# Pinning weight casts, weight differences and splits behind the operation traced last, and q and k evictions by ScalarE first

## The chip, the core and the metric

The kernel runs on one core of a Trainium2 chip. The metric is the time of one execution in microseconds, taken as the median of several runs. One execution is also recorded by the hardware profiler. The engines are PE (TensorE, matrix products), ACT (ScalarE), DVE (VectorE), POOL (GpSimd) and SP (SyncE, which here only starts transfers). PE's weight loads are shown as PEld.

## The reference

One decoder layer over 1024 tokens with 16 learned tokens ahead of them, so 1040 rows of 1024 numbers. In its core:

```python
a = rmsnorm(h, ln_mix_pre)
dq, dk, dv, hq, hf, hi, hg = split(a @ w_in)          # seven groups of 512 columns
y_diff = diff_attention(dq, dk, dv, ...)              # 4 heads, two softmax maps each, blocks of 128
y_hgrn = hgrn2(hq, hf, hi, hg, ...)                   # 4 heads, gated linear recurrence
h = h + rmsnorm(concat(y_diff, y_hgrn) @ w_out, ln_mix_post)
a = rmsnorm(h, ln_ffn_pre)
y = (gelu(gate) * up) @ w_down   # gate, up = depthwise conv of a @ w_up, width 3
h = h + rmsnorm(y, ln_ffn_post)
```

All is float32.

## The kernel before

**Three products for one.** Each float32 matrix product is made of three: both operands are split into a high part (`wh`, `ahi`: a cast to a narrower format) and the rest (`wl`, `alo`: the operand less its high part), and PE computes high by high, high by low, low by high. `split` (line 154) does it for weights: ACT casts, and POOL, or DVE where it is named, subtracts. `load_split` (line 158) starts a transfer of 128 by 512 weights into one of three buffers `wr` and splits it into `wh` and `wl`, of which there are four each.

**Order.** PE executes in the order in which the program is traced. The order on ACT, DVE, POOL and SP's queue is made by a planner: it walks the traced program with its own estimate of the durations, and an engine that comes free gets the earliest traced operation whose inputs it thinks ready. An operation that is ready early can thus be hoisted far ahead of what was traced before it. `tc.issue_after(x)` forbids that: what is traced inside on x's engine is put behind x in that engine's order. `V` and `A` are wrappers of DVE and ACT (class `Ordered`, line 46) which keep traced order in a few parts of the program; `G` is POOL itself.

**The stages.** From about 11 us the first projections begin. Up to about 530 us PE works through the columns of `w_in`, one tile of 128 columns after another, mixed with attention and HGRN: for each head h a stretch of four tiles for HGRN (`hf`, `hq`, `hi`, `hg`) beside attention of head h, then a stretch of three tiles for attention of head h + 1 (`dq`, `dk`, `dv`) beside HGRN of head h. `interleave` (line 60) does the mixing: it first takes 1500 units of dense work, then, for each piece of the side work, dense work worth a number of units; a matmul of 384 columns counts 161 units. When the side work is done, the rest of the dense work follows alone. A stretch is one call of `dense` (line 741). For each tile it calls `load_m`, that is, `load_split` twice, for the next tile; for the first tile of a stretch it calls it at the stretch's beginning. A tile has three groups of columns (272, 384 and 384 tokens), each of 24 matmuls into one of two PSUM banks `pi_...` (lines 232, 234, 236: the third product needs `wl`, the first two need only `wh`), and after each group an eviction:

- `ev_q`, `ev_k` (lines 593, 598): ACT and DVE write the two 64-row halves of q and k in turn, with their low parts.
- `ev_v`: ACT copies to `vt`, which is transposed (`to_nat`, `pn_va`) in the group after, when `flush` is called at the group's step 8. `ev_i` does the same with `ht` (`pn_vh`).
- `ev_g`: a sigmoid, which is ACT exponential, DVE minimum, ACT logarithm, ACT exponential on `sg`, then a DVE product for `gate`.

Attention (`attn`, line 611) takes blocks i of 128 tokens: `scores(i)`, `values(i)` (transposes `pt`, copies `at` and `az`) and `apply(i)` (products `pa`, line 709). HGRN (`hgrn_head`, line 402) has levels whose products `pl` (line 451) need DVE's products on `mix` and `kr`.

**Weight differences.** The down projection at the end uses seven products for eight, for which differences of quarters of `w_down` are needed. `down_sums` (line 187) makes them beside the stretches above: at each group `dense` takes one step of it. It loads four pieces `wd` (five buffers), subtracts four times on DVE and stores each to `tsc`, eleven times over.

**Output projection**, about 530 to 640 us: `out_first` (line 1013) multiplies the mixed rows by the first half of `w_out` and loads and splits the second half on the way (`load_wo(1, k)`, line 928, DVE subtracts), which a second pass uses later. HGRN of the last head runs beside it.

Of the kernel before, what the change touches and what calls it, by code (L numbers as in the profile page):

```python
# [9 lines left out]
F32 = mybir.dt.float32  # L10
# [3 lines left out]
ALU = mybir.AluOpType  # L14
# [12 lines left out]
NBLK = 9  # L27
# [18 lines left out]
class Ordered:  # L46
# [3 lines left out]
    def __getattr__(self, name):  # L50
        call = getattr(self.engine, name)

        def issue(*args, **kw):
            ins = call(*args, **kw)  # L54
            return self.tc.keep_in_program_order(ins) if self.state["ordered"] else ins

        return issue
# [29 lines left out]
def layer_kernel(ctx: ExitStack, tc: tile.TileContext, x, meta, table, lbl, gpre, gpost, win,  # L87
# [3 lines left out]
    V, A = Ordered(tc, nc.vector, state), Ordered(tc, nc.scalar, state)  # L91
    G, T, SY = nc.gpsimd, nc.tensor, nc.sync
# [52 lines left out]
    def ps_in(name):  # L145
        return pp.tile([P, 512], F32, tag="ip", name=name)

    def ps_m(name):
        return pp.tile([P, 512], F32, tag="m", name=name)
# [1 line left out]
    def ps_s(name):  # L151
        return pp.tile([P, 2, 512], F32, tag="S", name=name)

    def split(hi, lo, raw, eng=None):
        A.copy(hi, raw)
        (eng or G).tensor_tensor(lo, raw, hi.bitcast(F32), op=ALU.subtract)

    def load_split(src, name, where=None, bufs=4):
        raw = wp.tile([P, 512], F32, tag="wr", name=f"wr_{name}", bufs=3)
        hi = (where or wp).tile([P, 512], F32R, tag="wh", name=f"wh_{name}", bufs=bufs)  # L160
        lo = (where or wp).tile([P, 512], F32R, tag="wl", name=f"wl_{name}", bufs=bufs)
        last_load.append(SY.dma_start(raw, src))
        split(hi, lo, raw)
        return hi, lo

    def rstd_of(dst, ss, n):
# [20 lines left out]
    def down_sums():  # L187
        def load(k):
            with tc.issue_after(last_load[-1].ins):
                for nm, kk, half in (("11", k, 0), ("12", k, 1), ("22", k + NF // 2, 1), ("21", k + NF // 2, 0)):  # L190
                    b[nm] = wsp.tile([P, 512], F32, tag="wd", name=f"wd{nm}_{k}")
                    SY.dma_start(b[nm], wdown[P * kk: P * (kk + 1), 512 * half: 512 * (half + 1)])
            b["t3"] = wsp.tile([P, 512], F32, tag="wd", name=f"wd3_{k}")

        b = {}
        load(0)
        yield
        yield
        for k in range(NF // 2):
            for j, d, p_, q_ in ((2, "t3", "22", "12"), (0, "12", "12", "11"), (1, "22", "22", "12"), (3, "21", "21", "22")):  # L200
                V.tensor_tensor(b[d], b[p_], b[q_], op=ALU.subtract)
                with tc.issue_after(last_load[-1].ins):
                    SY.dma_start(tsc[j][P * k: P * (k + 1)], b[d])
                yield
            if k + 1 < NF // 2:
                load(k + 1)
                yield

    def up_raw(ft, nm):
# [7 lines left out]
    def load_m(m, name, where=None, bufs=4):  # L217
        return [load_split(win[m][:, 512 * c: 512 * (c + 1)], f"{name}_{c}", where, bufs) for c in range(2)]

    def proj_group(g, parts, name, evac):  # L220
        b0, b1 = GROUPS[g]
        t0, t1 = start(b0), start(b1 - 1) + P
        n = t1 - t0
        pt = ps_in(f"pi_{name}_{g}")
        for k in range(KD):
            yield from proj_step(pt[:, :n], parts, k, t0, t1, lambda: evac(g, b0, b1, t0, t1, pt[:, :n]))
# [171 lines left out]
    def flush():  # L398
        while late:
            to_nat(*late.pop(0))  # L400
# [183 lines left out]
    def attn_in(h):  # L584
        qs = [ap_.tile([P, L], F32R, tag=f"q{m}", name=f"q{m}_{h}") for m in range(2)]
        ks = [ap_.tile([P, L], F32R, tag=f"k{m}", name=f"k{m}_{h}") for m in range(2)]
        vn = ap_.tile([P, NBLK, P], F32, tag="avn", name=f"avn{h}")
        G.memset(vn[:, 0], 0.0)
        rr = ap_.tile([P, 256], F32, tag="rr", name=f"rr{h}")
        own = [slice(0, 64), slice(64, 128)]  # L590
        oth = [slice(64, 128), slice(0, 64)]

        def ev_q(g, b0, b1, t0, t1, pt):
            for m in range(2):
                A.mul(qs[m][own[m], t0:t1], pt[own[m]], 0.125)
                V.scalar_tensor_tensor(qs[m][oth[m], t0:t1], pt[own[m]], 0.125, qs[m][own[m], t0:t1].bitcast(F32), ALU.mult, ALU.subtract)

        def ev_k(g, b0, b1, t0, t1, pt):
            for m in range(2):
                A.copy(ks[m][own[m], t0:t1], pt[own[m]])  # L600
                V.tensor_tensor(kl[m][own[m], t0:t1], pt[own[m]], ks[m][own[m], t0:t1].bitcast(F32), op=ALU.subtract)
                A.copy(ks[m][oth[m], t0:t1], pt[own[m]])

        def ev_v(g, b0, b1, t0, t1, pt):
            vt = ap_.tile([P, 384], F32, tag="vt", name=f"vt{h}_{g}", bufs=1)
            A.copy(vt[:, : t1 - t0], pt)
            late.append((vn, vt, b0, b1, f"va{h}_{g}"))

        return (qs, ks, vn, rr), [(h, f"dq{h}", ev_q), (4 + h, f"dk{h}", ev_k), (8 + h, f"dv{h}", ev_v)]

    def attn(h, tens):
        qs, ks, vn, rr = tens
# [115 lines left out]
        for i in range(NBLK):  # L728
            if i + 2 < NBLK:
                ahead = scores(i + 2)  # L730
                yield next(ahead)
            yield from apply(i)
            if i + 2 < NBLK:
                yield from ahead
            if i + 2 == NBLK:
                yield 2
            if i + 1 < NBLK:
                yield from values(i + 1)
        carry.append(pend.pop("tail"))

    def dense(tiles, preload=None, side=iter(())):
        parts = preload
        for idx, (m, name, evac) in enumerate(tiles):
            if parts is None:
                parts = load_m(m, name)
            nxt = load_m(tiles[idx + 1][0], tiles[idx + 1][1]) if idx + 1 < len(tiles) else None
            for g in range(3):
                next(side, None)
                for step, c in enumerate(proj_group(g, parts, name, evac)):
                    if step == 8:  # L750
                        flush()
                    yield c
            parts = nxt
# [28 lines left out]
    pt = ps_m("pg")  # L782
# [80 lines left out]
    for c in range(2):  # L863
        raw = wp.tile([P, 512], F32, tag="wr", name=f"wr3_{c}", bufs=3)
# [60 lines left out]
    FIRST = (2, 3, 4, 5, 6, 7, 8, 1)  # L925
    kept = kpp.tile([P, 2, KD, P], F32R, tag="kept", name="kept")

    def load_wo(n, k):
        raw = wp.tile([P, 512], F32, tag="wr", name=f"wor{n}_{k}", bufs=3)
        last_load.append(SY.dma_start(raw, wout[P * k: P * (k + 1), 512 * n: 512 * (n + 1)]))  # L930
        if k < 2:
            where, tag, bufs = wp, ("wh", "wl"), 4
        elif n == 0 and k < KD - 1:
            where, tag, bufs = w0p, ("woh", "wol"), KD - 3
        else:
            where, tag, bufs = w1p, ("woh", "wol"), KD - 1
        hi, lo = (where.tile([P, 512], F32R, tag=t, name=f"{t}{n}_{k}", bufs=bufs) for t in tag)
        split(hi, lo, raw, V if n or k else G)
        return hi, lo

    def tok(i):
# [41 lines left out]
    wo = []  # L983
# [29 lines left out]
    def out_first():  # L1013
        pys = [ps_s(f"py0_{i}")[:, 0] for i in FIRST[:2]]
        for ks in ((0, 1), (2, 3)):
            for j in range(2):
                yield from out_part(sps[j], pys[j], wo0, ks[0] == 0, False, ks)
        sqs = [mix_split(i, 4, 7) for i in FIRST[:2]]
        for j in range(2):
            yield from out_part(sqs[j], pys[j], wo0, False, True)  # L1020
            if j == 0:
                sp_ = mix_split(FIRST[2], 0, 4)
            A.copy(y0[:, FIRST[j]], pys[j])
        for n, i in enumerate(FIRST[2:]):
            for k in ((0, 1), (2, 3), (4,), (5,), (6,), (7,))[n]:
                wo.append(load_wo(1, k))
            if n == 3:
                ahead.extend(mix_load(2, c) for c in range(4))
            py = ps_in(f"py0_{i}")
            sq_ = mix_split(i, 4, 7)  # L1030
            yield from out_part(sp_, py, wo0, True, False)
            if i != FIRST[-1]:
                sp_ = mix_split(FIRST[n + 3], 0, 4)
            yield from out_part(sq_, py, wo0, False, True)
            A.copy(y0[:, i], py)
        py = ps_in("py0_0")
        yield from out_meta(py, wo0, 7)
        A.copy(y0[:2, 0], py[:2])
        while 0 not in finished:
            yield None  # L1040
        for p in range(3):
            pre_last[p] = mix_split(p, 7, 8)
        for p in range(3):
            yield from out_last(p)
# [171 lines left out]
    for n, i in enumerate(order):  # L1216
# [5 lines left out]
        if i < 2:  # L1222
            m = (m0, kept)[i]
# [499 lines left out]
```

## Time and profile before

| | us |
|---|---|
| median of 3 runs | 1327.34 |
| lowest and highest | 1326.83, 1329.81 |
| profiled execution | 1325.77 |
| its span, first to last instruction | 1324.0 |

A row of waits reads: engine, tile and line that waited, the engine and tile that ended the wait, total us, times, longest. A row in order of time reads: start, duration, engine, line, operation, tile written `<-` tiles read, shape; in brackets the idle time of the engine before it and what ended it. All operations of ACT and DVE carry line L54, that of the wrapper, so they are told apart by their tiles. A PE matmul's duration includes its passage through the pipeline; the next one starts before it ends. PEclk is the clock granted to PE, 1.00 being full.

### The profile page before, as it was taken

How to read it: one execution, taken by the hardware profiler on the slowest of the kernel's cores; microseconds unless marked ns; L12 is line 12 of the kernel's file. 1: busy time of each engine (PE TensorE's matmuls, PEld its weight loads, DVE VectorE, ACT ScalarE, POOL GpSimd, SP SyncE). 2: the span in 40 equal slices, each digit the busy share in tenths (PEclk: the TensorE clock that was granted, in tenths of full speed). 3: DMA queues.
4: the chain of work that ended last, by engine and by line, in shares of the span. 5: the costliest groups of instructions: out<-in, count | busy, mean ns of one | idle time of the engine just before them, and what ended most of it. 6: DMA issues, size and time to landing. Idle time of an engine off the chain costs nothing.

```text
span 1324.0 us, 26317 instructions
## 1 busy us (share of the span) xinstructions
PE 1276.6 (96%) x10227; PEld 1181.8 (89%) x10227; DVE 912.8 (69%) x1589; ACT 689.4 (52%) x1670; POOL 413.5 (31%) x324
## 2 busy tenths in 40 slices
PE   6999999999999999999999799999999999999997
PEld 5898899989999999777899799999999998888886
DVE  7666557564756465834778777877787876697587
ACT  7465346535654565545665454554454454554454
POOL 3211211121202120112147567667667641010021
PEclk9999999999999999999999899999999999999999
DMA  6331323132311011835713222222222324964363
GB/s 217 109 127 61 101 94 132 56 129 77 124 44 35 33 33 46 262 114 182 242 41 112 84 84 76 92 80 82 81 89 76 105 85 166 343 222 156 107 207 120
DMA packets 84371, 153.07 MB, mean 116 GB/s; under 512 B 9571, under 2 KB 19843, under 8 KB 84246
## 3 DMA queue, kind: packets, MB, share of 16 engines
q1 hardware_dynamic: 84246, 151.39, 34.0%
q8 instruction: 80, 1.31, 0.4%
q14 instruction: 45, 0.37, 0.1%
HBM read 112.69 MB, written 38.67 MB: 114 GB/s over the span
## 4 chain that ended last, share of the span: by engine, by line
PE 71%; DVE 6%; DMA 3%; ACT 3%; issue 2%; POOL 1%; SPq 1%; DVEq 0%; ACTq 0%; POOLq 0%
PE pd L1534 5%; PE pd L1535 5%; PE pd L1533 5%; PE pb L1336 4%; PE pb L1337 4%; PE pb L1338 4%; PE pa L1337 2%; PE pa L1336 2%; PE pa L1338 2%; PE pa L709 2%; PE pc L1338 2%; PE pc L1337 2%; PE pc L1336 2%; PE py L970 2%; PE py L974 2%
## 5 line engine op out<-in xcount | busy, mean ns | idle before, releaser
L1336 PE MATMUL pb<-t,uh 128*128 128x258 f32 (+1 forms) x480 | 135.4, 282 | 10.7 <-DVE u L54 10.7
L1337 PE MATMUL pb<-t,uh 128*128 128x258 f32 (+1 forms) x480 | 135.1, 281 | 0.0
L1338 PE MATMUL pb<-t,ul 128*128 128x258 f32 (+1 forms) x480 | 134.9, 281 | 0.0
L1534 PE MATMUL pd<-wl,gh 128*128 128x512 f32 (+1 forms) x314 | 121.4, 386 | 0.5 <-DVE wl L54 0.5
L1535 PE MATMUL pd<-wh,gl 128*128 128x512 f32 (+1 forms) x314 | 120.6, 384 | 0.0
L1533 PE MATMUL pd<-wh,gh 128*128 128x512 f32 (+1 forms) x314 | 120.1, 383 | 0.0
L54 DVE SCALAR_TENSOR_TENSOR c<-uu,cwt,c 128x512 f32<-128x512 f32 x88 | 92.4, 1050 | 22.5 <-ACT c L54 21.9
L1291 POOL TENSOR_TENSOR c<-c,c 128x512 f32<-128x512 f32 x44 | 68.4, 1554 | 124.1 <-ACT c L54 118.1
L1336 PEld LDWEIGHTS pb<-t,uh 128*128 128x128 f32 x480 | 91.5, 191 | 11.3 <-DVE u L54 11.3
L1337 PEld LDWEIGHTS pb<-t,uh 128*128 128x128 f32 x480 | 91.6, 191 | 0.0
L1338 PEld LDWEIGHTS pb<-t,ul 128*128 128x128 f32 x480 | 91.4, 190 | 0.0
L1337 PE MATMUL pa<-t,uh 128*128 128x258 f32 (+1 forms) x320 | 89.8, 281 | 0.0
L1338 PE MATMUL pa<-t,ul 128*128 128x258 f32 (+1 forms) x320 | 89.7, 280 | 0.0
L1336 PE MATMUL pa<-t,uh 128*128 128x258 f32 (+1 forms) x320 | 89.7, 280 | 0.0
L54 DVE SCALAR_TENSOR_TENSOR c<-ug,cwt,c 128x512 f32<-128x512 f32 x88 | 87.6, 996 | 1.7 <-ACT c L54 1.1
L1338 PE MATMUL pc<-t,ul 128*128 128x256 f32 x320 | 88.3, 276 | 0.0
L1336 PE MATMUL pc<-t,uh 128*128 128x256 f32 x320 | 88.3, 276 | 0.0
L1337 PE MATMUL pc<-t,uh 128*128 128x256 f32 x320 | 88.3, 276 | 0.0
L1534 PEld LDWEIGHTS pd<-wl,gh 128*128 128x128 f32 x314 | 59.0, 188 | 13.6 <-DVE wl L54 1.6
L1533 PEld LDWEIGHTS pd<-wh,gh 128*128 128x128 f32 x314 | 58.9, 188 | 12.6
L1535 PEld LDWEIGHTS pd<-wh,gl 128*128 128x128 f32 x314 | 59.0, 188 | 11.5
L54 ACT ACTIVATE pb<-S,ast 128x528 f32<-128x528 f32 (+7 forms) x72 | 46.5, 647 | 39.1 <-DVE ast L54 38.9
(411 smaller groups left out, 4210.3 us busy)
## 6 DMA issues: line engine op xcount, KB each, us to landing
ra<-in_wup_dram SPq DMA_DIRECT2D x80, 256.0 KB, 2.7
wd<-in_wdown_dram SPq DMA_DIRECT2D x44, 256.0 KB, 4.2
tsc<-wd SPq DMA_DIRECT2D x44, 256.0 KB, 2.7
gsc<-c SPq DMA_DIRECT2D x44, 256.0 KB, 2.0
wi<-tsc SPq DMA_DIRECT2D x44, 256.0 KB, 2.8
gi<-gsc SPq DMA_DIRECT2D x33, 256.0 KB, 3.7
wi<-in_wdown_dram SPq DMA_DIRECT2D x33, 256.0 KB, 3.0
msc<-mm SPq DMA_DIRECT2D x21, 256.0 KB, 3.5
```

What stands on the lines that cost most here:

```text
L54: ins = call(*args, **kw)
L709: T.matmul(po[:, :P], w_, vn[:, j], start=(j == 0), stop=(j == i))
L970: T.matmul(py[:r], mh[:, j, :r], hi, start=(first and j == 0), stop=False)
L974: T.matmul(py[:r], ml[:, j, :r], hi, start=False, stop=(last and k == k1 - 1))
L1291: G.tensor_tensor(cg, cg, cu, op=ALU.mult)
L1336: T.matmul(pt, hi[:, s], th[:, k], start=(first and k == 0), stop=False, skip_group_check=True)
L1337: T.matmul(pt, hi[:, s], tl[:, k], start=False, stop=False, skip_group_check=True)
L1338: T.matmul(pt, lo[:, s], th[:, k], start=False, stop=(k == 3), skip_group_check=True)
L1533: T.matmul(py, gh[:, s], wh, start=(k == 0 and pr not in (3, 7)), stop=False, skip_group_check=True)
L1534: T.matmul(py, gh[:, s], wl, start=False, stop=False, skip_group_check=True)
L1535: T.matmul(py, gl[:, s], wh, start=False, stop=(k == NH - 1), skip_group_check=True)
```

## The change

- The wrapper remembers the operation traced last on its engine, and `in_turn(engine)` puts what is traced inside behind it in that engine's order.
- The ACT casts in `load_split` are pinned so; POOL's subtraction is not. `split` called from elsewhere is not pinned.
- The DVE subtractions of `down_sums` are pinned so, and after each load there is one more step before the next four.
- In `ev_q` both ACT scalings come before both DVE operations, in `ev_k` all four ACT copies before both DVE subtractions.
- In attention's last blocks there are more pauses, in which dense work is taken: one more unit before the last `apply`, and three for two after the one before.
- `flush` is called at step 14 of a group, not at step 8.
- The splits of the second half of `w_out` are traced one step later than their loads and pinned on ACT and on DVE.

```diff
@@ class Ordered
             ins = call(*args, **kw)
+            self.last = ins
             return self.tc.keep_in_program_order(ins) if self.state["ordered"] else ins
@@
-    def split(hi, lo, raw, eng=None):
-        A.copy(hi, raw)
-        (eng or G).tensor_tensor(lo, raw, hi.bitcast(F32), op=ALU.subtract)
+    def in_turn(eng):
+        return tc.issue_after(eng.last.ins)
+
+    def split(hi, lo, raw, eng=None, turn=()):
+        with ExitStack() as st:
+            for e in turn:
+                st.enter_context(in_turn(e))
+            A.copy(hi, raw)
+            (eng or G).tensor_tensor(lo, raw, hi.bitcast(F32), op=ALU.subtract)
@@ load_split
-        split(hi, lo, raw)
+        split(hi, lo, raw, turn=(A,))
@@ down_sums
-                V.tensor_tensor(b[d], b[p_], b[q_], op=ALU.subtract)
+                with in_turn(V):
+                    V.tensor_tensor(b[d], b[p_], b[q_], op=ALU.subtract)
...
                 load(k + 1)
+                yield
                 yield
@@ ev_q
                 A.mul(qs[m][own[m], t0:t1], pt[own[m]], 0.125)
+            for m in range(2):
                 V.scalar_tensor_tensor(qs[m][oth[m], t0:t1], pt[own[m]], 0.125, ...)
@@ ev_k
                 A.copy(ks[m][own[m], t0:t1], pt[own[m]])
+                A.copy(ks[m][oth[m], t0:t1], pt[own[m]])
+            for m in range(2):
                 V.tensor_tensor(kl[m][own[m], t0:t1], pt[own[m]], ...)
-                A.copy(ks[m][oth[m], t0:t1], pt[own[m]])
@@ attn
+            if i + 1 == NBLK:
+                yield 1
             yield from apply(i)
...
             if i + 2 == NBLK:
-                yield 2
+                yield 3
@@ dense
-                    if step == 8:
+                    if step == 14:
                         flush()
@@ load_wo, out_first
+    held = []
-    def load_wo(n, k):
+    def load_wo(n, k, hold=False):
...
-        split(hi, lo, raw, V if n or k else G)
+        if hold:
+            held.append((hi, lo, raw, V))
+        else:
+            split(hi, lo, raw, V if n or k else G)
...
         for n, i in enumerate(FIRST[2:]):
+            while held:
+                split(*held.pop(0), turn=(A, V))
             for k in ((0, 1), (2, 3), (4,), (5,), (6,), (7,))[n]:
-                wo.append(load_wo(1, k))
+                wo.append(load_wo(1, k, True))
...
+        while held:
+            split(*held.pop(0), turn=(A, V))
         py = ps_in("py0_0")
```

## Prediction

> **What bounds the kernel now.** I read the page's head first, then busy time by stage, then what the tensor engine (PE) waits for in the stages that the change touches.
>
> ```profile
> span 1324.0 us, 26317 instructions
> PE 1276.6 (96%) x10227; PEld 1181.8 (89%) x10227; DVE 912.8 (69%) x1589; ACT 689.4 (52%) x1670; POOL 413.5 (31%) x324
> ```
>
> PE is the bound, and it runs in traced order, so nothing but a shorter or longer PE wait can move the time. The same busy times for the two touched stages (columns: PE, weight loads, DVE, ACT, POOL, clock, DMA share, GB/s): input projections with attention and HGRN from 58 to 530 us, output projection from 530 to 640 us.
>
> ```profile
> 58.00:530.00 472.00, 455.54 (x4245) 433.77 (x4245) 285.57 (x655) 250.03 (x737) 79.86 (x82) 1.00 0.24 82
> 530.00:640.00 110.00, 107.73 (x931) 82.29 (x930) 63.82 (x128) 59.17 (x164) 20.93 (x18) 1.00 0.61 194
> ```
>
> PE idles 472.00 - 455.54 = 16.5 us in the first and 2.3 us in the second. The waits of PE in the first (total, times, longest), then the two largest of the second, then the largest of the stage before, 18 to 58 us:
>
> ```profile
> PE pl L451 <- DVE mix L54: 4.8, 4, 2.5
> PE pt L685 <- DVE at L54: 2.3, 4, 1.0
> PE pa L709 <- ACT pb L54: 1.9, 3, 0.8
> PE pa L709 <- DVE at L54: 1.7, 3, 1.3
> PE pi_dv L232 <- ACT k L54: 1.5, 3, 0.5
> PE pn_vh L347 <- ACT mix L54: 1.0, 3, 0.3
> PE pn_vh L347 <- ACT pb L54: 0.9, 1, 0.9
> PE pi_hf L232 <- ACT k L54: 0.8, 1, 0.8
> PE pi_dk L232 <- DVE q L54: 0.4, 1, 0.4
> ```
>
> ```profile
> PE pl L451 <- DVE mix L54: 0.8, 1, 0.8
> PE pl L451 <- DVE am L54: 0.6, 1, 0.6
> ```
>
> ```profile
> PE pi_dv L232 <- DVE q L54: 1.7, 1, 1.7
> ```
>
> The reader is to see two things. Every wait is short, and each names an engine that is far from full: these are waits of order, where DVE or ACT did something else first. And no row has `wh` or `wl`: **the weight casts never hold PE now**. All that the change can win here is this list.
>
> **What it may win.** Evictions of q and k, beside head 0:
>
> ```profile
> 60.76 2.37 DVE L54 TENSOR_TENSOR wd<-wd,wd 128x512 f32<-128x512 f32 x2
> ```
>
> ```profile
> 63.63 0.96 ACT L54 CAST k<-pi_dk 64x384 fp32r<-64x384 f32 x2 [2.86 <-DVE kl L54]
> 65.29 0.47 ACT L54 CAST k<-pi_dk 64x384 fp32r<-64x384 f32 x1 [0.70 <-DVE kl L54]
> ```
>
> ```profile
> 64.66 0.34 PE L236 MATMUL pi_dv<-ahi,w 128*128 128x384 f32 x1
> 65.81 0.39 PE L232 MATMUL pi_hf<-ahi,wh_hf 128*128 128x272 f32 x1 [0.82 <-ACT k L54]
> 66.17 0.29 PE L236 MATMUL pi_hf<-ahi,wl_hf 128*128 128x272 f32 x1
> ```
>
> ACT and DVE take turns on one PSUM bank; each turn may find DVE in a weight difference (`wd`, two of them 2.37 us here). With ACT's four k copies (or two q scalings) first, ACT waits for DVE no more and DVE is needed once. The same instructions remain. This should remove the waits `pi_dv <- ACT k` and `pi_dk <- DVE q`, 1.9 us (between 0 and 1.9). The 0.8 of `pi_hf` falls into a boundary that I cost below. Of the 1.7 us at `pi_dv <- DVE q` I count 0.5: DVE is full there and its next product is what PE would wait for.
>
> A wait costs more than its idle time: from 64.66 to 65.81 is 1.15 us where matmuls otherwise follow in some 0.13 (66.17 is the third within 0.36), so 0.82 idle is 1.0 of delay, 0.2 more.
>
> Weight differences:
>
> ```profile
> L54 DVE TENSOR_TENSOR wd<-wd,wd 128x512 f32<-128x512 f32 x44 | 34.7, 788 | 15.0 <-DMA wd<-in_wdown_dram 11.4 <-issue 2.2 <-DMA wr_hi<-in_win_dram 0.9
> ```
>
> 44 subtractions of 788 ns, run as soon as the planner thinks their data there; DVE stands 11.4 us waiting for DMA with the HGRN products queued behind. Pinned, and one group later after each load, they come one to a group of 24 matmuls. The work is the same, 34.7 us on an engine busy 285.57 of 472. The loads and the 44 stores keep their places behind the last weight load on SP's queue; stores come later by as much, and the down projection reads them hundreds of us on, so I cost them at nothing. Of the 4.8 at `pl <- DVE mix` I take 4.0 (0 to 4.8).
>
> Attention's waits (`pt`, `pa`: 2.3 + 1.9 + 1.7 = 5.9 us) have several causes, casts and differences in front of ACT's and DVE's copies among them; I take 4.0 (0 to 5.9). The later flush (step 14 for 8) gives ACT six matmuls more for its copy before the transposes `pn_vh`: 1.9 gone (0 to 1.9). The added pauses near the last block only put some ten dense matmuls ahead of `pa` and leave fewer for the end: nothing, since the same matmuls are issued. Output weight splits, one step later: 0.8 of the 1.4 shown (0 to 1.4); their consumers come in the next pass over the tokens, which hides the delay.
>
> Sum: 1.9 + 0.5 + 4.0 + 4.0 + 1.9 + 0.8 = 13.1 us of idle, and 0.2 for each of some 17 waits, 3.4: 16.5. Against it I set 1.5 for new small waits (each pinned DVE operation now stands behind one that may wait; 44 of them, a handful hit): **15 us gained**. The bounds: the evictions and the flush alone, 3.8 and eight times 0.2, are 5; all the rows but `pi_hf`, 17.6, and their 24 times 0.2, are 22.
>
> **What it costs: the casts of the first tile of each stretch.** `load_split` is called at the start of a tile for the next one, but for the first tile of each `dense` it is called there and then: `hf` after `dv`, `dq` after `hg`. The cast is hoisted today. For the `hf` that PE starts at 196.71, ACT cast its second half 20 us before, and POOL subtracted at once:
>
> ```profile
> 176.45 0.62 ACT L54 CAST wh_hf<-wr_hf 128x512 fp32r<-128x512 f32 x1
> ```
>
> ```profile
> 177.15 1.29 POOL L156 TENSOR_TENSOR wl_hf<-wr_hf,wh_hf 128x512 fp32r<-128x512 f32 x1 [2.12 <-ACT wh_hf L54]
> ```
>
> ```profile
> 196.53 0.34 PE L236 MATMUL pi_dv<-ahi,wl_dv 128*128 128x384 f32 x1
> ```
>
> ```profile
> 196.96 0.29 PE L236 MATMUL pi_hf<-ahi,wl_hf 128*128 128x272 f32 x1
> ```
>
> ```profile
> 197.36 0.47 ACT L54 COPY vt<-pi_dv 128x384 f32<-128x384 f32 x1
> ```
>
> Pinned, the cast follows the last ACT operation traced, and that is the eviction `vt<-pi_dv` of the group that PE has just finished; PE has nothing else in its order, since a stretch begins with its own matmuls. So: PE ends 196.53 + 0.34 = 196.87; crossing 0.05 (ACT's k ends 65.29 + 0.47 = 65.76, PE starts 65.81); copy 0.47; cast 0.62; crossing 0.08 (177.07 to 177.15); POOL 1.29; crossing 0.05. The first L236 of `hf` starts at 199.43, not 196.96; less 0.1 by which ACT operations overlap, **2.4 us**. The two matmuls that need only the cast run inside that gap. The second half's subtraction ends 1.29 later, while PE has nine matmuls of 0.13 and two more to do: no second wait. Three such boundaries: 7.2. At head 0 the same sum from 64.66 gives 67.56 against 66.17, 1.3 with the overlap, since today's wait there ends in the same place.
>
> `dq` after `hg` is worse, as the eviction is a sigmoid whose third ACT operation is the last traced. PE around it, and the sigmoid of the group before:
>
> ```profile
> 272.69 0.34 PE L236 MATMUL pi_hg<-ahi,wl_hg 128*128 128x384 f32 x1
> ```
>
> ```profile
> 273.11 0.29 PE L236 MATMUL pi_dq<-ahi,wl_dq 128*128 128x272 f32 x1
> ```
>
> ```profile
> 268.84 0.49 ACT L54 ACTIVATE sg<-pi_hg 128x384 f32<-128x384 f32 x1 [0.18 <-PE pi_hg L236]
> 269.76 0.62 ACT L54 ACTIVATE sg<-sg,one 128x384 f32<-128x384 f32 x1 [0.43 <-DVE sg L54]
> 270.42 0.53 ACT L54 ACTIVATE sg<-sg 128x384 f32<-128x384 f32 x1
> ```
>
> The chain takes 270.95 - 268.84 = 2.11 us. From PE's end at 273.03: 0.05 + 2.11 + 0.62 + 0.08 + 1.29 + 0.05 = 4.20, so 277.23 against 273.11; less the overlap, **4.0 us**, three times: 12.0. Together 7.2 + 1.3 + 12.0 = **20.5 us lost**, between 16 (a fifth regained, where later products find the work of DVE and ACT done sooner) and 22 (DVE's part of the sigmoid late by 0.5 each time). The inner tiles' casts, also later, are hidden: each is used a whole tile of 72 matmuls after it can run, and no row above shows one waited for. The last stretch's `wo0` splits are not pinned.
>
> **Sum.** 20.5 - 15 = +5.5 on a span of 1324.0, hence 1329.5. The profiled execution took 1325.77, 1.77 around its span, and the median of the runs is 1327.34, 1.57 more: 1327.34 + 5.5 = **1333** for the median.
>
> **Rivals.**
> *The waits removed weigh as much as the new ones.* If every PE wait shown goes, 22 us against 20.5, the time is 1326; it decides from 17.8 us removed on, and only with the new gaps at their lower end of 16 is it measurably faster, 1321. For it: all rows are waits of order. Against: those in attention recur where ACT runs its own exponentials.
>
> *The pin does not put the casts on the path*, if the planner can still issue them early (it does what it says on inner tiles alone). Then 15 us remain as gain: 1312. Against it: the operation pinned to cannot start before PE's last matmul, and ACT is one stream.
>
> *The clock falls in the new gaps.* In the longest wait of the trace the clock halved (last number but two):
>
> ```profile
> 728.00:730.00 2.00, 1.24 (x11) 1.04 (x10) 2.00 (x2) 1.06 (x4) 1.58 (x1) 1.00 0.08 31
> 732.00:734.00 2.00, 0.00 (x0) 0.00 (x0) 2.00 (x3) 2.00 (x5) 1.80 (x1) 0.55 0.00 0
> 736.00:738.00 2.00, 0.56 (x2) 0.56 (x3) 1.71 (x4) 0.92 (x2) 0.21 (x1) 0.50 0.65 215
> 742.00:744.00 2.00, 2.00 (x17) 2.00 (x16) 0.85 (x2) 0.62 (x1) 1.92 (x3) 0.89 0.00 0
> ```
>
> PE stopped at 729.24 (728 + 1.24), the clock was at half from about 732.2 (0.55 as the mean of that row), PE resumed at 737.44, and the clock came back about 742.4: 5 us at half, 2.5 lost. A `dq` gap is 4.2 us long with two matmuls in it, longer than the 3.0 before that fall; if all three fall, 7.5 us: 1340.5. Against: the two matmuls, and the gap must cover the clock's own interval. The Trainium skill (TensorE: Matmul & The Clock Gate, Part 1) says that the gate looks at free-running windows of about 3.4 us and halves after an idle one; by that, a fall in such a gap is a matter of phase. The trace agrees as far as a fall 3.0 us after PE stopped.
>
> **How the numbers follow.** Forecast (slower by 3 to 12) 0.54; clock falls as well 0.12; removed waits about equal or more 0.19 (0.14 within 0.2%, 0.05 faster); casts off the path 0.15. 0.2% of this time, 2.7 us, is about what a measurement tells from no change. Slower 0.66, same 0.14, faster 0.20. The likeliest case's own range is 1330 to 1339; that for 8 in 10 runs from 1315 to 1342, leaving out part of the off-path case and of the clock case.
>
> **What would show it.** Right: new PE waits `pi_hf <- POOL wl_hf` or `<- ACT wh_hf` (four places, 1.3 and 2.4 us) and `pi_dq <- wl_dq` (three of 4.0), PE idle 4 to 8 us above 16.5 between 58 and 530; `pn_vh`, `pi_dv <- ACT k` gone; `wd` no longer waiting for DMA. Wrong: the casts of `wh_hf` still 20 us ahead of their use; or half clock after those gaps; or a different length of the 8 us stop at 729, which the change doesn't touch but whose order the same planner makes.

## The result, and the profile after

| | kernel before | changed kernel |
|---|---|---|
| median, us | 1327.09 | 1349.15 |
| range of the runs, us | 1326.38 to 1329.81 | 1348.66 to 1350.83 |
| span of the profiled execution, us | 1324.0 | 1347.5 |

The ratio is 1.0179, 95% interval 1.0158 to 1.0199: slower by 22 us by the medians of the table and by 24 by the ratio (21 to 26 by its interval). The head of the page of the changed kernel, with the granted clock in 40 slices:

```profile
span 1347.5 us, 26321 instructions
...
PE 1288.5 (96%) x10227; PEld 1191.9 (88%) x10227; DVE 914.7 (68%) x1589; ACT 689.2 (51%) x1670; POOL 409.0 (30%) x324
...
PEclk9999999989999999999999899999999999999999
```

PE runs as many matmuls as before, and DVE, ACT and POOL are busy within 5 us of what they were. The same stage as before, 58 to 530 us:

```profile
58.00:530.00 472.00, 443.34 (x4105) 421.20 (x4104) 274.45 (x627) 238.48 (x705) 79.80 (x83) 0.98 0.24 80
```

PE idles 472.00 - 443.34 = 28.7 us in it, 12.2 more than before, and the clock, 1.00 before, is 0.98 as a mean. By 530 us PE has done 4105 matmuls of this stage, where it had done 4245. What PE waits for between 58 and 545 us, all rows:

```profile
PE pi_dq L241 <- ACT wh_dq L54: 8.0, 3, 2.7
PE pi_hf L241 <- ACT wh_hf L54: 4.4, 4, 1.1
PE pi_hf L245 <- POOL wl_hf L163: 3.4, 4, 0.9
PE pa L720 <- DVE at L54: 2.7, 3, 1.1
PE pi_dq L245 <- POOL wl_dq L163: 2.6, 3, 1.0
PE pn_vh L356 <- ACT pb L54: 1.9, 3, 1.3
PE pn_va L354 <- ACT kn L54: 1.9, 3, 0.6
PE pt L696 <- DVE at L54: 1.8, 3, 1.0
PE pl L460 <- DVE mix L54: 1.3, 3, 0.6
PE pa L720 <- ACT pb L54: 0.6, 2, 0.3
PE pt L696 <- ACT pb L54: 0.5, 1, 0.5
PE pt L696 <- ACT vn L54: 0.5, 2, 0.3
```

Four rows are new and have `wh` or `wl` in them: 8.0 + 4.4 + 3.4 + 2.6 = 18.4 us at seven places. The row `pl <- DVE mix` fell from 4.8 to 1.3 and `pi_dv <- ACT k` is gone; `pn_vh` is as long as it was, 1.9, but waits for `pb` alone, and `pn_va` is new. One boundary of each kind. At the second `hf`, PE first, then ACT (x2: the casts of both halves in one row):

```profile
198.59 0.39 PE L241 MATMUL pi_hf<-ahi,wh_hf 128*128 128x272 f32 x1 [1.09 <-ACT wh_hf L54]
...
199.95 0.39 PE L245 MATMUL pi_hf<-ahi,wl_hf 128*128 128x272 f32 x1 [0.85 <-POOL wl_hf L163]
```

```profile
197.54 0.48 ACT L54 COPY vt<-pi_dv 128x384 f32<-128x384 f32 x1
197.91 1.14 ACT L54 CAST wh_hf<-wr_hf 128x512 fp32r<-128x512 f32 x2
```

At the first `dq` behind an `hg`, PE first, then POOL:

```profile
143.47 0.40 PE L241 MATMUL pi_dq<-ahi,wh_dq 128*128 128x272 f32 x1 [2.68 <-ACT wh_dq L54]
...
144.82 0.60 PE L245 MATMUL pi_dq<-ahi,wl_dq 128*128 128x272 f32 x1 [0.83 <-POOL wl_dq L163]
```

```profile
143.50 2.51 POOL L163 TENSOR_TENSOR wl_dq<-wr_dq,wh_dq 128x512 fp32r<-128x512 f32 x2 [6.80 <-ACT wh_dq L54]
```

The reader is to see the order: eviction, cast, subtraction, product, one after the other, with PE idle twice, the two products that need the cast alone between. The second `dq` row shows another thing: its matmul took 0.60, where the one behind the same wait at `hf` took 0.39. The clock had halved. Windows of 3.41 us on each side of that moment, and of the one at the third `hf` (the last number but two is the clock):

```profile
141.17:144.58 3.41, 0.52 (x2) 0.30 (x2) 0.92 (x2) 2.83 (x6) 1.08 (x1) 1.00 0.12 44
144.58:147.99 3.41, 3.17 (x23) 2.92 (x27) 0.00 (x0) 0.49 (x1) 2.66 (x3) 0.50 0.63 178
...
332.32:335.73 3.41, 1.49 (x9) 0.96 (x8) 0.56 (x1) 2.53 (x7) 1.77 (x2) 1.00 0.00 0
335.73:339.14 3.41, 3.41 (x18) 3.41 (x17) 0.36 (x2) 0.00 (x0) 1.98 (x2) 0.50 0.75 242
```

After the gap at 334 PE starts 18 matmuls in a window, and 27 in the next one. Such halves follow five of the seven gaps, four of 3.41 us and one of 6.83, 20.5 us together; at half speed that is up to 10.2 us of work.

### The profile page after: what moved, and what is told of

It reads as the page before. It is cut to its first block, busy times and chain, and to the rows that moved or that the text cites. A ratio compares the mean times of both kernels' runs of the same rounds, so it can differ in the third digit from the quotient of the medians.

```text
span 1347.5 us, 26321 instructions
## 1 busy us (share of the span) xinstructions
PE 1288.5 (96%) x10227; PEld 1191.9 (88%) x10227; DVE 914.7 (68%) x1589; ACT 689.2 (51%) x1670; POOL 409.0 (30%) x324
## 4 chain that ended last, share of the span: by engine, by line
PE 66%; issue 17%; DVE 7%; ACT 5%; POOL 3%; DMA 2%; SPq 0%; DVEq 0%; POOLq 0%; ACTq 0%
PE pd L1556 5%; PE pd L1557 5%; PE pd L1555 5%; PE pb L1358 4%; PE pb L1359 4%; PE pb L1360 4%; PE pa L1359 3%; PE pa L1358 3%; PE pa L1360 3%; PE pc L1358 2%; PE pc L1360 2%; PE pc L1359 2%; PE py L988 2%; PE py L990 2%; PE py L992 2%
## 5 line engine op out<-in xcount | busy, mean ns | idle before, releaser
L1192 POOL TENSOR_TENSOR ws<-ra,ra 128x512 f32<-128x512 f32 x40 | 58.6, 1466 | 14.2 <-DMA ra<-in_wup_dram 11.4
```

The source lines that it names most:

```text
L1192: G.tensor_tensor(sums[nm], a, b, op=op)
```

## The experiments

Two theories stood at the start. A has three parts: the waits for the pinned first casts (some 20 us), the half clock that these gaps set off (some 10), and a gain of some 8 from all else. B has the waits alone, with the half clock free of charge and no gain. C, that the other edits lose, was kept as a third. All ratios are to the kernel before, run on the same chip.

### The first tiles' casts free; no cast pinned; only the casts pinned

```diff
# first tiles free, against the changed kernel; load_split takes turn=(A,) unless told otherwise
-                parts = load_m(m, name)
+                parts = load_m(m, name, turn=())
# no cast pinned, against the changed kernel
-        split(hi, lo, raw, turn=(A,))
+        split(hi, lo, raw)
# only the casts pinned, against the kernel before
+        with tc.issue_after(A.last.ins):
             split(hi, lo, raw)
```

> The changed kernel with one thing undone: the casts of the first tile of each stretch (hf after dv, dq after hg) are not pinned; those of the inner tiles still are. Theory A (three parts: 20.2 us of new waits at the seven boundaries, some 10 us of half clock that those waits set off, and a gain of some 8 us from the rest): both losses go, so 1317 to 1321 us, with no half clock between 58 and 530 us and no wait of PE on wh or wl there. Rival B (the waits are the whole loss, the half clock costs nothing since PE would have waited anyway, and the rest gains nothing): 1349 - 20 = 1329. Rival C (the rest of the change loses by itself): above 1329.

> The changed kernel with no weight cast pinned at all; all else stays. It differs from the run with the first tiles free only in the inner tiles. If pinning the inner casts is what keeps them from standing in front of evictions and attention's copies, this run is 2 to 4 us slower than that one, with the waits pt and pa on ACT back. If the inner pins do nothing, the two agree within 1 us: 1317 to 1321 by theory A, 1329 by rival B.

> The kernel before with the one edit that load_split's ACT cast is pinned. Theory A: 1327 + 20 of waits + 10 of half clock, less 1 to 3 for casts that no longer stand ahead of evictions: 1353 to 1357. Rival B: 1327 + 20 = 1347. Rival C: 1340 or less, since part of the loss would be the other edits'.

| | median, us | ratio, 95% interval |
|---|---|---|
| first tiles free | 1322.71 | 0.9965 (0.995 to 0.9981) |
| no cast pinned | 1320.34 | 0.9954 (0.9939 to 0.9969) |
| only the casts pinned | 1352.66 | 1.0201 (1.018 to 1.0222) |

The seven first casts are the whole loss. With them free, no row of PE's waits has `wh` or `wl`, the clock is 1.00 from 58 to 530 us, and the change is 4.6 us faster than the kernel before (0.0035 of 1327); with them pinned it is 23.8 slower, so their pin costs 28.4. That is more than the 20 of waits, which speaks against B; and the rest of the change gains, which rules out C. The gain is smaller than A had it in one run (1322.71 for 1317 to 1321) and near it in the other. With no cast pinned the gain is 6.1 us, and the two runs don't differ beyond their intervals, so pinning the inner tiles' casts shows nothing here. The pin alone is at the lower edge of A's 1353 to 1357, and B's 20 us would be a ratio of 1.015, outside its interval. It has the same four rows as the changed kernel, 18.0 us:

```profile
PE pi_dq L234 <- ACT wh_dq L54: 8.1, 3, 2.7
PE pi_hf L234 <- ACT wh_hf L54: 4.4, 4, 1.1
PE pi_hf L238 <- POOL wl_hf L157: 3.3, 4, 0.8
...
PE pi_dq L238 <- POOL wl_dq L157: 2.2, 3, 0.8
```

### The gaps filled with matmuls that nobody reads

```diff
# in dense, at the first group of the first tile of a stretch
+                    for _ in range(20 if name[0] == "d" else 8):
+                        T.matmul(d[:, :272], ahi[:, 0, :P], ahi[:, 0, :272], start=True, stop=True)
...
+                    if first and step == 1:
+                        for _ in range(6):
+                            T.matmul(d[:, :272], ahi[:, 0, :P], ahi[:, 0, :272], start=True, stop=True)
```

The second version takes one more PSUM tile, `d2`, for the six.

> The changed kernel with PE kept busy in the seven gaps: matmuls on operands that are long there, into a PSUM bank that nobody reads, 20 (after hg) or 8 (after dv) ahead of the first product and 6 between the second and the third, of about 0.13 us each, so that they end before the cast and the subtraction do. The waits for the cast stay as they are. Theory A: the clock stays full at the boundaries and the time falls by the half clock's part, 8 to 11 us, to 1338 to 1341. Rival B: no change, 1349, or longer if the extra matmuls delay the real ones.

> As the run with the gaps filled, but with two PSUM tiles for the extra matmuls, so that the groups after them keep the banks that they have in the changed kernel. Theory F (the half clock costs about 10 us; the first such run gave half of it back in the tile hq, because the odd number of extra tiles changed what later evictions and the planner met): no half clock between 58 and 530 us, and the tile hq as long as in the changed kernel, so 9 to 11 us off the changed kernel's 1349, 1338 to 1340, ratio about 1.009 to 1.010 to the kernel before. Rival G (the half clock is worth only the 5.5 us that the first run showed): 1343 to 1344 again, ratio 1.013.

Measured: 1343.7 us, ratio 1.0127 (1.011 to 1.0145), and with two tiles 1341.22, ratio 1.0115 (1.0098 to 1.0132). The clock stays full in both. The second version, at the first `dq`:

```profile
142.00:144.00 2.00, 1.82 (x15) 1.60 (x14) 0.56 (x1) 1.97 (x5) 0.59 (x1) 1.00 0.00 0
144.00:146.00 2.00, 1.89 (x16) 1.67 (x15) 0.00 (x0) 0.37 (x1) 2.00 (x3) 1.00 0.26 33
```

The casts come as late as before (this one starts at 142.72, and at 142.82 in the changed kernel). The two versions gain 6.9 us (0.0052) and 8.5 (0.0064); by the second version's interval and the changed kernel's the gain lies between 5 and 12. Both miss what was expected, 1338 to 1341 and 1338 to 1340, by 1 to 3 us, and the interval of the second leaves both of its theories open.

These gains are not the half clock alone, as the starts of the tiles show. The tile `dq` of this boundary, from its first product to that of `dk`, in the changed kernel:

```profile
143.47 0.40 PE L241 MATMUL pi_dq<-ahi,wh_dq 128*128 128x272 f32 x1 [2.68 <-ACT wh_dq L54]
...
161.35 0.29 PE L241 MATMUL pi_dk<-ahi,wh_dk 128*128 128x272 f32 x1
```

The same in the second version:

```profile
143.38 0.39 PE L241 MATMUL pi_dq<-ahi,wh_dq 128*128 128x272 f32 x1 [0.18 <-ACT wh_dq L54]
...
159.90 0.29 PE L241 MATMUL pi_dk<-ahi,wh_dk 128*128 128x272 f32 x1
```

That is 17.88 us against 16.52. Measured so, the five tiles behind the gaps that had halved the clock take 90.0 us in the changed kernel, 82.8 in the first version and 83.2 in the second. The half clock there thus costs some 7 us, 7.2 and 6.8, and theory B is out. But the tiles `hq` behind the second, third and fourth `hf` take 4.7 and 5.4 us longer than in the changed kernel, and the output projection, where the changed kernel's clock fell a sixth time (last section), is 0.9 and 2.0 shorter up to its first product on `pz`. (The profiled executions took 1345.22 and 1345.4, which is above the medians, so the traces do not show all of the gain.) The even number of tiles did not bring `hq` back, so that reason falls: in both versions PE waits more in attention there, of which the largest row is this one of the second version (2.7 in the changed kernel):

```profile
PE pa L720 <- DVE at L54: 4.2, 6, 1.2
```

Either the planner orders ACT and DVE otherwise when the extra matmuls are in the program, or work that was late behind the half clock now waits for DVE. Which, stays open.

### The other edits, undone one at a time

All four start from the kernel with no cast pinned (ratio 0.9954).

```diff
# flush
-                    if step == 14:
+                    if step == 8:
# order: A, V, A, A, V, A again in ev_k, and A, V, A, V in ev_q
# differences
-                with in_turn(V):
-                    V.tensor_tensor(b[d], b[p_], b[q_], op=ALU.subtract)
+                V.tensor_tensor(b[d], b[p_], b[q_], op=ALU.subtract)
...
-                yield
# pauses
-            if i + 1 == NBLK:
-                yield 1
...
-                yield 3
+                yield 2
```

> The kernel with no weight cast pinned (1320.3 us, against 1327.3 for the kernel before), with the flush back at step 8. Theory D (the late flush loses: its transposes now ask for a PSUM bank while attention's exponentials still read it, 4.0 us of waits pn_vh and 1.5 pn_va against 1.9 before): 1317 to 1318.5. Rival E (the late flush gains the 1.9 us that the prediction counted): 1321 to 1323.

> The kernel with no weight cast pinned, with the q and k evictions in their old order. Theory D (the new order only trades the wait of pi_dv on ACT's k, 1.5 us, for one on DVE's kl, 2.0 us, and gains some 1 to 2 us at head 0): 1321 to 1322. Rival E (it gains the 1.9 + 0.5 us counted and more, since DVE is asked for once): 1323 to 1325.

> The kernel with no weight cast pinned, with the weight differences neither pinned nor one group later. Both theories give it the largest single gain: waits pl on mix go from 2.1 back to about 4.8 and DVE's waits for DMA return, 1323 to 1325. If it is nothing, 1320, the gain of the whole comes from elsewhere.

> The kernel with no weight cast pinned, with the old pauses near attention's last blocks. The prediction costs them at nothing: 1319.5 to 1321, with the same waits pt and pa at the last blocks. If they matter, a wait at pa of the last block appears and the run is 2 us or more off.

| undone | median, us | ratio, 95% interval | worth of the edit by it |
|---|---|---|---|
| flush at 14 | 1315.08 | 0.9917 (0.9904 to 0.993) | 4.9 us lost |
| q and k order | 1326.91 | 1.0008 (0.9998 to 1.0019) | 7.2 us gained |
| differences | 1326.75 | 1.0004 (0.9995 to 1.0013) | 6.6 us gained |
| pauses | 1317.24 | 0.9932 (0.9921 to 0.9944) | 2.9 us lost, intervals overlap |

The four sum to 6.0 gained, about the 6.1 of the whole. That need not mean that they add: the order and the differences shorten the same row, `pl <- DVE mix`, which is 2.1 us with both new, 3.2 with the old order and 3.1 with the old differences.

The **flush** loses, for a reason that its kernel's trace shows (no cast pinned, flush at 14; ACT, then PE):

```profile
501.54 0.68 ACT L54 ACTIVATE pb<-E,ast 128x512 f32<-128x512 f32 x1
```

```profile
502.37 0.44 PE L356 MATMUL pn_vh<-ident,ht 128*128 128x128 f32 x2 [1.35 <-ACT pb L54]
```

At step 14 the transposes take a PSUM bank of the kind `m` that the scores `E` of attention's last blocks still occupy, and wait for ACT's exponential to leave it. At step 8 they came before those scores. That kernel has `pn_vh <- ACT pb` at 4.0 us and `pn_va <- ACT kn` at 1.5; with the flush at 8 there remain:

```profile
PE pn_vh L356 <- ACT mix L54: 1.0, 3, 0.3
...
PE pn_vh L356 <- ACT pb L54: 0.3, 1, 0.3
```

The **order** was worth far more than either theory had. With the old order beside pinned differences, PE waits longer for the last k copy than it did in the kernel before (1.5 us), and the wait at head 0 (1.7) is back:

```profile
PE pi_dv L241 <- ACT k L54: 5.5, 3, 1.8
```

With the new order the row is `pi_dv <- DVE kl`, 2.0: less than 5.5, but no less than the 1.5 of the kernel before. The **differences** behave as foretold on DVE. The DVE group of all 44, with the old placing and with the new (both no cast pinned):

```profile
L54 DVE TENSOR_TENSOR wd<-wd,wd 128x512 f32<-128x512 f32 x44 | 34.1, 775 | 16.1 <-DMA wd<-in_wdown_dram 15.6
```

```profile
L54 DVE TENSOR_TENSOR wd<-wd,wd 128x512 f32<-128x512 f32 x44 | 33.3, 756 | 0.4
```

DVE no longer stands waiting for a transfer with other products behind it. On PE the worth is only in part where it was expected: with the old placing `pl <- DVE mix` is 3.1, not 4.8, and attention has a row that the kernel with the new placing lacks:

```profile
PE pa L718 <- DVE at L54: 2.2, 4, 1.3
```

For the **pauses** both kernels have the same rows at attention's last blocks, and the wait at the last `pa` that the expectation named did not come. One row differs, in the output projection: with the new pauses PE waits there for a split of the first half of `w_out`, with the old ones it doesn't.

```profile
532.46 0.50 PE L988 MATMUL py<-woh,mm 128*128 128x512 f32 x1 [1.16 <-ACT woh L54]
```

From the first product of the output projection to the first on the tile `kept` it is 47.5 us with the new pauses and 45.5 with the old, which is most of the 2.9. Why the pauses delay that split is not shown, and as the intervals overlap, whether they cost anything isn't settled.

### Towards a better version

All have the flush at 8 and the old pauses.

```diff
# output splits old, against flush and pauses old
-                wo.append(load_wo(1, k, True))
+                wo.append(load_wo(1, k))
# handed over, against the inner casts pinned
-        parts = preload
+        parts = handed.pop() if handed else preload
...
+            if then and idx + 1 == len(tiles):
+                handed.append(load_m(*then))
```

> No weight cast pinned, flush at step 8, old pauses: of the change there remain the q and k order, the weight differences and the output splits. If the two losses found (late flush about 5 us, pauses about 3) add up, 1311 to 1313 us. If they overlap in the same waits at the end of attention, 1314 to 1316.

> As the run with flush and pauses old, but with the inner tiles' casts pinned (the first tile of each stretch is free). Theory: inner pins are nearly nothing on PE's path, within 1.5 us of that run either way. Rival (the prediction's: casts stood ahead of attention's copies, some 2 to 4 us): faster than it by 2 or more.

> As the run with flush and pauses old, but with the splits of the second half of w_out as before. The prediction gave them 0.8 us; the waits shown between 530 and 650 us were 2.3 before and 1.7 in the changed kernel. So 0 to 1 us slower than that run; a wait py on ACT woh should go.

> As the run with the inner casts pinned, and now the first tile of a stretch is loaded at the start of the last tile of the stretch before, as every inner tile is, and its cast is pinned too (the very first stretch alone is free as before). Theory (a pin costs only where the cast is traced when PE is about to need it): no wait on wh or wl, no half clock, within 1.5 us of the run with the inner casts pinned. Rival (pinned casts as such cost, by holding weight buffers or by standing behind waiting evictions): 5 to 20 us slower than it.

| | median, us | ratio, 95% interval |
|---|---|---|
| flush and pauses old | 1314.13 | 0.9908 (0.9893 to 0.9923) |
| inner casts pinned | 1316.12 | 0.9922 (0.991 to 0.9935) |
| output splits old | 1315.01 | 0.9917 (0.9905 to 0.993) |
| pinned and handed over | 1312.69 | 0.99 (0.9886 to 0.9913) |

The first is within its own error of the kernel with the flush alone undone (0.9917): the two losses overlap, or the pauses are none. By their times, inner pins (2.0 us slower by the medians) and output splits (0.9) are not to be told from nothing. Their traces do differ. With the inner casts pinned attention has a row `pa <- DVE at` of 2.6 us that the first lacks, and `pl <- DVE mix` is 1.3 for 2.1. With the output splits old a wait `pl <- DVE mix` of 2.3 stands in the output projection, the clock is at 0.50 from 540 to 542 us behind it, and the way to the first product on `kept` is 3.4 us longer. The last pins every cast, as the changed kernel does, except at the very first stretch, and hands each stretch's first tile to the stretch before. No row of PE's waits has `wh` or `wl`, the clock is full, and PE idles 9.9 us in the stage where the changed kernel idles 28.7:

```profile
58.00:530.00 472.00, 462.09 (x4410) 440.74 (x4409) 298.31 (x669) 255.93 (x748) 79.76 (x82) 1.00 0.27 87
```

It is 13 us faster than the kernel before and the fastest of all, though its interval overlaps that of the first. It was expected within 1.5 us of the run with the inner casts pinned and is 3.4 faster; the rival, 5 to 20 us slower because pinned casts cost as such, is out. So a pin by itself costs nothing that these runs can tell; it costs where the cast is traced when PE is about to need it.

## Why the prediction was right and wrong

The direction was right, and the main step: the pinned cast of a stretch's first tile lands on PE's path. The time, 1333, was 16 us short: 1349 lies outside both of its ranges, 1330 to 1339 and 1315 to 1342. Two steps failed: the clock, which the sum left full, and the gain, of which 15 us were counted and some 6 measured.

- *New waits, 20.5 us.* Right. 18.4 of idle shown, less the 0.8 that stood at `pi_hf` before, and 0.2 for each of the 14 times that PE starts again, is 20.4; the gaps are for one `hf` 1.09 + 0.85 and for one `dq` 2.68 + 0.83, as worked out link by link.
- *The clock stays full.* Wrong; this was a rival at 0.12, of three `dq` gaps and 7.5 us. The clock fell after all three and after two `hf` gaps, which the rival left out. By the five tiles behind these gaps that cost some 7 us.
- *A gain of 15 us.* This is the larger miss: with no cast pinned the rest gave 6.1. By its terms:
  - The flush, +1.9, was a loss of 4.9, since I looked at when ACT's copy is ready and not at whose bank the transposes take. The pauses, 0, are perhaps -2.9.
  - Attention, 4.0, came to nothing in the changed kernel: its rows `pt` and `pa`, 5.9 before, are 6.1 (2.7 + 1.8 + 0.6 + 0.5 + 0.5). The differences were the cause of one of them: `pa <- DVE at`, 1.7 before, is gone with no cast pinned and back at 2.2 with the old differences. But pinning the inner casts brings such a row again, 2.6 with the first tiles free and 2.7 in the changed kernel.
  - The output splits, 0.8, are within the error of the times.
  - Two terms were too small: the order of q and k, 2.4, measured 7.2, and the differences, 4.0 at `pl`, measured 6.6, of which `pl` shows 1.0. Part of this the bare list of the kernel before cannot show: with the differences pinned, the old order's wait for the last k copy is 5.5 us and not 1.5. What either edit is worth alone no run shows.

With the clock's 7 and a gain of 6.1 for 15, the prediction's own sum, 20.5 - 15, becomes 20.5 + 7 - 6.1 = 21.4, against 23.8 measured (interval 21 to 26). Two slips in it change nothing: the upper bound counts 24 waits where its rows have 25, and the list of waits leaves out a row of 0.5, `ssa <- DVE ona`.

The Trainium skill (TensorE: Matmul & The Clock Gate, Part 1) has the clock halve after an idle window of about 3.4 us. The trace agrees in that the halves come in pieces of 3.41, 6.83 and, from 755.56 us, 10.24 us, multiples of one window; it differs on what sets them off, since windows in which PE was partly busy did so too (last section).

## What to carry to other kernels

An order edge is only as cheap as the place where the operation is traced: before pinning something that a planner hoists, find the first use behind it at every call, the first call of a loop above all, and move the call earlier if that use is next. When an operation on PSUM is moved, check which bank it takes there and who still reads it, not only when its input is ready. A list of waits gives the size of what is waited for now; edits that shift the same engines have to be measured together and one by one.

## What the runs showed of the hardware

A gap need not be long to halve the clock. The fall at 335.73 follows 3.41 us in which PE was busy 1.49, and its two idle pieces were some 1.1 and 0.8 us; that at 144.58 follows 0.52 of busy time in 3.41. The gap of the second `hf`, about as long (1.09 + 0.85 at 198.59), set off nothing. All the falls and recoveries shown here lie on one grid of 3.41 us, and on that grid the gap of the second `hf` is spread over two windows, busy 2.24 and 2.66. So by this trace a gap of 2 us counts or not by where it falls on the grid. Windows on it that were busy 1.17 to 1.49 of 3.41 were followed by half clock:

```profile
274.29:277.70 3.41, 1.17 (x7) 0.84 (x5) 0.45 (x2) 1.75 (x4) 0.00 (x0) 1.00 0.00 0
...
414.24:417.65 3.41, 1.44 (x9) 1.22 (x10) 0.56 (x1) 2.10 (x5) 2.24 (x2) 1.00 0.00 0
...
468.85:472.26 3.41, 1.47 (x9) 0.94 (x8) 1.16 (x2) 2.57 (x7) 1.73 (x2) 1.00 0.00 0
```

One more fall, at 561.01, followed a wait of 1.5 us of the output projection (`py <- ACT woh`), in a window busy 2.02 by the records, while a window busy 1.87 was not followed by one:

```profile
410.83:414.24 3.41, 1.87 (x11) 1.54 (x9) 0.47 (x2) 1.08 (x2) 0.00 (x0) 1.00 0.15 57
557.60:561.01 3.41, 2.02 (x8) 1.17 (x9) 2.26 (x5) 2.27 (x4) 0.00 (x0) 1.00 0.99 332
```

So these busy times alone do not draw the border; where exactly it lies, these runs don't tell.
